# Slots of 576 columns, norm roots through DRAM, and a changed order at three places of a decoder layer

## The chip, the cores and the metric

The kernel runs on one core of one Trainium2 chip. The metric is the device time of one execution in microseconds (us). The kernel before takes 971.31 us (median of 3 runs, 971.28 to 971.34). The core has five engines with queues of their own: TensorE (PE in the profile; its weight loads are listed as PEld), VectorE (DVE), ScalarE (ACT), GpSimd (POOL) and SyncE (SP). Here SP only issues DMAs; POOL and ACT issue some as well.

## The reference

One layer of a hybrid decoder works on a prompt of 512 tokens and on 8 samples of 4 tokens each, with 1024 features. Cut to what the change touches:

```python
def _layer(x, ...):
    m, ... = _mixer(_rmsnorm(x, norm_mix_pre), ...)
    x = x + _rmsnorm(m, norm_mix_post)
    f, ... = _conv_ffn(_rmsnorm(x, norm_ffn_pre), ...)
    return x + _rmsnorm(f, norm_ffn_post), ...

def _rmsnorm(x, g):
    return x * rsqrt(mean(x * x, -1) + EPS) * g

def _mixer(h, ...):
    xr, q, k, v, g_lru, g_attn = split(h @ w_in)      # 1024, 1024, 256, 256, 1024, 1024 columns
    lru  = _rg_lru(_causal_dwconv(xr), ...)            # log_a = -8 * r * softplus(-lam)
    attn = _band_attention(q, k, v, ...)               # window 128, 8 query heads, 2 kv heads, bias, sinks
    return (sigmoid(g_lru) * (lru @ w_lru_o) + sigmoid(g_attn) * (attn @ w_attn_o)) @ w_out, ...
```

The samples attend over a cache of 128 keys and values each. Outputs are the two token arrays, the recurrent and convolution states and the key and value windows, all float32.

## The kernel before

**Tiles.** Activations lie with features on the 128 partitions and the 544 tokens (512 of the prompt, 32 of the samples) along the columns. A tile of that kind takes one of 53 slots of 568 columns (`SLOT`), so a slot is 2272 bytes long on each partition and every second one starts at an odd multiple of 32 bytes. Weights lie in `raw_*`, `wh_*`, `wl_*` tiles. Each float32 operand is split into a high and a low part (`hH`, `hL` of the normed input; `wh_in`, `wl_in` of the weights), and a product is three matmuls: high by high, low by high, high by low. DVE and ACT make the parts.

**Steps and ticks.** Work is cut into steps of one 128-column block of a weight matrix against one half of the tokens: 8 feature blocks by 3 products, 24 matmuls on 256 columns (half a=0) or 288 columns (half a=1), into one of three PSUM banks (`psm`; names `pm_first`, `pmin`). Behind each step stands a tick: it advances a clock by 1 and runs the side work that has become due. Side work is written as generators; `yield n` means that the next piece becomes due n ticks later (1 without a number). Lists named `mids`, `after`, `late` and `last` hold pieces for set places around a tick; the function given to `step` as `done` is such a piece and takes the finished bank. The order on PE, ACT, DVE and POOL in this part is exactly the order in which the code is written; each engine runs its own queue in order.

**Norm.** The input projection uses x times the gain. The reciprocal root of the mean square of each token is applied later: `rep` holds it, repeated on all partitions, and DVE multiplies it into the k, v, xr and gate columns (`scaled`, L171); q doesn't take it there, since the scores are scaled with `rq`. `norms` collects the squares in `ss` (one column for each block of tokens) and calls `roots` for the first two blocks (256 tokens) and later for the other three (288 tokens): DVE lays the roots on a diagonal (`dg`), a matmul of PE with `ones` spreads them over the partitions into `ps_rep`, and ACT copies that to `rep` (L554). A second small matmul into the same bank, `ohp` by `relx`, gives the rows of the bias table; they go by `rvec`, `rscr` and `rrep` through DRAM to the tables `btab` (L661, L686, L692, DMAs of POOL).

**Order of the blocks.** `qkv_order` lists the blocks of 128 columns: 8 to 15 are the query heads, 16 and 17 the keys, 18 and 19 the values. The first one is a step of its own (`pm_first`), and its `done` is put off by way of `after` and `mids`.

**Decay.** `params` computes the decay `cc`, `cneg` of the recurrence as a series, some 23 small instructions on POOL (L624 to L636). POOL also issues the DMAs `xdram` (L518), `kout`, `vout`, `knt`, `vnt` and `btab`.

**Samples.** `sample_attn(g)`, g = 0 and 1, loads cache rows, turns the keys by DVE (`kcT`, L893), and PE takes them for the scores `pss`.

**The end.** Finished features `ft` go out in three ways: the first token blocks come from PE in token order (`fg`, L1979), block 3 and half of block 2 are turned by PE (`yo`, L1887), the other half of block 2 is turned by DVE and leaves as 16 small DMAs (`yb_p`, L1866, list `pieces`, emptied by `send`), and the samples leave as 4 DMAs of POOL (`yb_s`, L1850, `samples_out`) once `y_blocks` has turned the last `ft`. The order there is written out at L2009 to L2043.

Of the kernel before, what the change touches and what calls it, by code (L numbers as in the profile page):

```python
# [11 lines left out]
F32 = mybir.dt.float32  # L12
F32R = mybir.dt.float32r
AF = mybir.ActivationFunctionType
ALU = mybir.AluOpType
# [31 lines left out]
SLOT = 568  # L47
# [76 lines left out]
def hawk_step(ctx, tc, I, O):  # L124
# [15 lines left out]
    cp = mixer.enter_context(tc.tile_pool(name="mixer_const", bufs=1))  # L140
    mixer.enter_context(tc.manual_schedule(engines={act.engine, dve.engine, pool.engine}))
# [16 lines left out]
    def SM(name, shape, tag="sm"):  # L158
        return smp.tile(shape, F32, tag=tag, name=name)
# [76 lines left out]
    qkv_order = (16, 18, 8, 9, 10, 11, 17, 19, 12, 13, 14, 15)  # L236
# [107 lines left out]
    def step(key, X, a, done, target=None, look=2, quick=False):  # L344

        first_ = key == order[0] and a == 0
        ps = first_ps if first_ else PM("pm" + "_".join(str(z) for z in key) + f"_{a}")
        if first_:
            pass
        elif quick:  # L350
            mmhalf(ps, key, X, a, range(4))
            now[0] += 0.5
            sides()
            mmhalf(ps, key, X, a, range(4, 8))
            done(a, ps)
        elif len(wunits) <= 2 * FIRST and a == 0 and key in order[1:FIRST]:
            mmhalf_low_last(ps, key, X, a)
        else:
            mmhalf(ps, key, X, a)
        tick(upto(key, a, look) if target is None else target, 0.5 if quick else 1)  # L360
        if first_:
            after.append(lambda: mids.insert(1, lambda: done(a, ps)))
        elif not quick:
            (last if len(wunits) <= 2 * FIRST and a == 0 else late).append(lambda: done(a, ps))
# [6 lines left out]
    rows_a = cp.tile([96, P], F32, name="rows_a")  # L371
# [31 lines left out]
    pvn = keep.tile([P, 24], F32, name="pvn")  # L403
# [25 lines left out]
    ss = cp.tile([P, 4, 5], F32, name="ss")  # L429
    dve.memset(ss, 1.0)  # L430
# [105 lines left out]

    def roots(i0, i1):
        dg = T(f"dg_{i0}")
        t0 = TOK[i0][0]
        spans = [(TOK[i][0] - t0, TOK[i][1], i) for i in range(i0, i1)]  # L540
        n = spans[-1][0] + spans[-1][1]
        last.append(lambda: xrstd(i0, i1))
        for o, w, i in spans:
            last.append(lambda o=o, w=w, i=i: dve.tensor_scalar(dg[:, o:o + w], ident[:, :w], ss[:, 1, i:i + 1], None,
                                                                ALU.mult))
        yield

        def spread_roots():
            ps = PX(f"ps_rep{i0}")
            mm(ps[:, 0:n], ones, dg[:, 0:n], True, True)  # L550
            if not i0:
                mm(ps[:NH, 256:256 + WIN], relx, ohp, True, True)
                ps_ohp.append(ps)
            act.copy(rep[:, t0:t0 + n], ps[:, 0:n])  # L554

        if i0:
            spread_roots()
        else:
            mids.insert(0, spread_roots)

    def norms():
        xsquare(0, 1, True)
        yield from roots(0, 2)
        yield
# [17 lines left out]
    rows_f = cp.tile([P, 2, P], F32, name="rows_f")  # L582
# [24 lines left out]
    def params():  # L607
# [15 lines left out]
        yield  # L623
# [255 lines left out]
    def sample_attn(g):  # L879
# [9 lines left out]
        yield 2  # L889
# [962 lines left out]
    def y_blocks(c):  # L1852
# [8 lines left out]
        if c == 3:  # L1861
            dst = yp[2 * P:3 * P, 0:512].rearrange("(b q) (c a d) -> a b q c d", b=4, a=4, d=32)
            src = yb["p"][:, 0:512].rearrange("p (b c d) -> p b c d", b=4, c=4)
            for a in range(4):
                for b in range(4):
                    pieces.append(lambda a=a, b=b: nc.sync.dma_start(out=dst[a, b], in_=src[32 * a:32 * a + 32, b]))  # L1866
            send(10)

    def send(n):
        for f in pieces[:n]:  # L1870
            f()
        del pieces[:n]
# [138 lines left out]
    r0 = rstd(0)  # L2011
    ps = tokens(1, 0)
# [3 lines left out]
    send(3)  # L2016
    gain = tokens_done(1, 0, ps)
    tokens_out(0, r0, 1)()
    send(len(pieces))
    while todo or side:  # L2020
        slot(0)
    samples_out()
# [56 lines left out]
```

## Time and profile before

| what | before |
|---|---|
| median of 3 runs | 971.31 us |
| the profiled execution | 971.4 us |
| its span in the trace | 969.6 us |
| instructions | 20080 |
| PE busy | 959.3 us, 99% of the span, 7598 matmuls |
| DVE busy | 762.3 us, 79% |
| ACT busy | 550.3 us, 57% |
| POOL busy | 166.3 us, 17% |
| granted TensorE clock, mean | 0.999 |
| HBM traffic | 118.21 MB read, 16.74 MB written, 139 GB/s |

All times of trace rows count from the start of the span; 1.8 us of the profiled execution lie outside it. A row of the timeline gives the start and the length of one instruction or of a run of like ones ("x3"), engine, line, operation, output and inputs without buffer numbers, and in brackets the idle time of the engine before it, with what ended it. Matmuls overlap, so the step from one start to the next, not the length shown, is what each takes from PE. "SPq", "ACTq" and the POOL rows of DMAs are the issue of a transfer, not the transfer itself.

### The profile page before, as it was taken

To read this page: it belongs to the slowest core of one execution; us is meant where nothing else is said; L and a number is where in the kernel's file an instruction comes from. 1 tells how busy PE (TensorE), PEld (TensorE's weight loads), DVE (VectorE), ACT (ScalarE), POOL (GpSimd) and SP (SyncE) were. 2 spreads that over 40 slices of the span, in tenths; PEclk is the share of its full clock that TensorE was granted. 3 is DMA by queue.
4 is the path that set the end of the run, shared out by engine and by line. 5 is a ranking of instruction groups with operands and counts; after the bars stand their busy time and mean duration, and the time that the engine had idled before them with its cause. 6 is when DMAs were issued, how large, how long until landed. Compare 5 with 4: busy or idle time off the path is not lost.

```text
span 969.6 us, 20080 instructions
## 1 busy us (share of the span) xinstructions
PE 959.3 (99%) x7598; PEld 951.6 (98%) x7598; DVE 762.3 (79%) x1626; ACT 550.3 (57%) x1342; POOL 166.3 (17%) x283
## 2 busy tenths in 40 slices
PE   9999999999999999999999999999999999999997
PEld 8999999999999999999999999999999999999996
DVE  5778888857858555689967878787888888888886
ACT  6544433467476425566867665555556565656642
POOL 2152000003406231230011110101011111111023
PEclk9999999999999999999999999999999999999999
DMA  7885436533334537235147575767667675859543
GB/s 221 235 240 164 149 90 155 157 94 88 92 104 152 172 102 196 66 124 178 46 108 196 132 188 141 183 154 171 166 154 195 143 200 135 203 130 234 178 147 92
DMA packets 247596, 147.26 MB, mean 152 GB/s; under 512 B 36324, under 2 KB 231788, under 8 KB 247468
## 3 DMA queue, kind: packets, MB, share of 16 engines
q1 hardware_dynamic: 237468, 124.15, 43.5%
q0 software_dynamic: 9824, 19.55, 12.0%
q10 hardware_dynamic: 208, 2.30, 0.6%
q8 instruction: 59, 0.97, 0.4%
q14 instruction: 37, 0.30, 0.1%
HBM read 118.21 MB, written 16.74 MB: 139 GB/s over the span
## 4 chain that ended last, share of the span: by engine, by line
PE 92%; DVE 5%; ACT 1%; issue 1%; DMA 0%; DVEq 0%; SPq 0%; POOL 0%; ACTq 0%; POOLq 0%
PE pmin L165 20%; PE pmdn L165 17%; PE pux L1531 16%; PE puy L1531 8%; PE pq L1531 6%; PE pmlo L165 5%; PE pmao L165 5%; PE pmout L165 4%; PE puz L1531 4%; PE pg L165 1%; PE pvp L165 1%; PE psc L165 1%; PE ptok L165 1%; DVE wl_e L168 1%; DMA pt<-pd 0%
## 5 line engine op out<-in xcount | busy, mean ns | idle before, releaser
L165 PE MATMUL pmin<-hH,wh_in 128*128 128x256 f32 (+1 forms) x568 | 163.9, 291 | 0.0
L165 PE MATMUL pmin<-hL,wh_in 128*128 128x256 f32 (+1 forms) x568 | 162.4, 288 | 0.0
L165 PE MATMUL pmin<-hH,wl_in 128*128 128x256 f32 (+1 forms) x568 | 159.1, 288 | 0.0
L165 PE MATMUL pmdn<-fH,wh_dn 128*128 128x256 f32 (+1 forms) x448 | 129.2, 288 | 0.0
L165 PE MATMUL pmdn<-fH,wl_dn 128*128 128x256 f32 (+1 forms) x448 | 128.8, 287 | 0.0
L165 PE MATMUL pmdn<-fL,wh_dn 128*128 128x256 f32 (+1 forms) x448 | 128.7, 287 | 0.0
L165 PEld LDWEIGHTS pmin<-hH,wh_in 128*128 128x128 f32 x568 | 107.2, 189 | 1.4 <-issue 1.2
L165 PEld LDWEIGHTS pmin<-hL,wh_in 128*128 128x128 f32 x568 | 107.2, 189 | 0.1
L165 PEld LDWEIGHTS pmin<-hH,wl_in 128*128 128x128 f32 x568 | 104.7, 188 | 0.2 <-issue 0.2
L177 DVE SCALAR_TENSOR_TENSOR uc<-u,fv,uc 128x560 f32<-128x560 f32 x128 | 101.9, 796 | 1.7 <-ACT uc L1562 1.2
L165 PEld LDWEIGHTS pmdn<-fH,wl_dn 128*128 128x128 f32 x448 | 84.4, 188 | 0.0
L165 PEld LDWEIGHTS pmdn<-fL,wh_dn 128*128 128x128 f32 x448 | 84.3, 188 | 0.1
L165 PEld LDWEIGHTS pmdn<-fH,wh_dn 128*128 128x128 f32 x448 | 84.2, 188 | 0.1
L1659 ACT COPY u<-pux 128x272 f32<-128x272 f32 x52 | 20.1, 386 | 87.2 <-PE pux L1531 87.2
L168 DVE TENSOR_TENSOR u<-puy,u 128x240 f32<-128x240 f32 (+2 forms) x78 | 24.6, 343 | 48.1 <-PE puy L1531 30.5
L174 DVE TENSOR_TENSOR ft<-ft,pmdn 128x256 f32<-128x256 f32 (+1 forms) x104 | 45.0, 433 | 16.6 <-PE pmdn L165 16.4
L283 ACT ACTIVATE wh_in<-raw_in 128x512 fp32r<-128x512 f32 x70 | 42.2, 624 | 21.3 <-issue 12.1
L290 DVE TENSOR_TENSOR wl_in<-raw_in,wh_in 128x512 fp32r<-128x512 f32 x70 | 47.8, 693 | 1.0 <-ACT wh_in L283 1.0
L1562 ACT ACTIVATE uc<-u,fv 128x560 f32<-128x560 f32 x64 | 48.1, 755 | 0.0
L781 ACT ACTIVATE s<-s,st 128x256 f32<-128x256 f32 (+1 forms) x32 | 15.2, 476 | 54.5 <-DVE st L778 43.2
L168 DVE TENSOR_TENSOR wl_dn<-raw_dn,wh_dn 128x512 fp32r<-128x512 f32 x56 | 38.3, 683 | 3.2 <-ACT wh_dn L1480 3.2
L1469 POOL DMA_DIRECT2D raw_up_s<-raw_up_s x26 | 22.0, 848 | 92.6 <-DMA raw_up_s<-raw_up__11280 5.5
(745 smaller groups left out, 3368.7 us busy)
## 6 DMA issues: line engine op xcount, KB each, us to landing
raw_in<-in_w_in_dram SPq DMA_DIRECT2D x35, 512.0 KB
raw_dn<-in_w_down_dram SPq DMA_DIRECT2D x56, 256.0 KB
raw_up_s<-in_w_up_dram SPq DMA_DIRECT2D x25, 512.0 KB
raw_up_s<-raw_up_s POOLq DMA_DIRECT2D x26, 256.0 KB, 4.2
raw_ao<-in_w_attn_o_dram SPq DMA_DIRECT2D x8, 512.0 KB
raw_lo<-in_w_lru_o_dram SPq DMA_DIRECT2D x8, 512.0 KB
raw_out<-in_w_out_dram SPq DMA_DIRECT2D x8, 512.0 KB
pd<-pb SPq DMA_DIRECT2D x12, 256.0 KB
```

What stands on the lines that cost most here:

```text
L165: pe.matmul(out, l, r, start=start, stop=stop)
L168: dve.tensor_tensor(out=out, in0=a, in1=b, op=ALU.subtract)
L174: dve.tensor_tensor(out=out, in0=a, in1=b, op=ALU.add)
L177: dve.scalar_tensor_tensor(out=out, in0=a, scalar=s_, in1=b, op0=op0, op1=op1)
L283: act.activation(hl[0], raw, AF.Copy)
L290: (eng or dve).tensor_tensor(out=hl[1], in0=raw, in1=f32(hl[0]), op=ALU.subtract)
L781: act.activation(s3[:, j, :], s3[:, j, :], AF.Exp, bias=ng[:, j:j + 1], accum_out=sm[:, j:j + 1])
L1469: pool.dma_start(out=w["p4"], in_=w["p2"], accum_op=ALU.add)
L1531: pe.matmul(ps[:, :HN], w, x, start=start and k == 0 and i == 0, stop=stop and k == 3 and i == 2, skip_group_check=True)
L1562: act.activation(yt[j][:, 0:FLATU], u[:, 0:FLATU], AF.Copy, scale=fv[:, j:j + 1])
L1659: act.copy(e[nm_], z)
```

## The change

1. **Slots.** `SLOT` goes from 568 to 576 columns (2304 bytes); the small tiles of the tags `sm` and `st` get a pool of their own for the mixer, `rows_a` and `rows_f` become parts of one temporary tile `rows`, and `pvn` and `ss` are padded to 32 columns. With that all operands start at multiples of 64 bytes.
2. **Order of the blocks.** Three query heads come ahead of the first keys and values, and the first step's `done` is no longer put off.
3. **Roots.** `dg`, its matmuls and the copies to `rep` go. DVE turns `ss` (`ssT`), POOL writes each block's roots into a row in DRAM (`rrow`), and one more DMA of POOL reads the row back into all partitions of `rep`. The matmul for the bias rows stays, with a bank of its own (`ps_ohp`).
4. **Decay.** The series starts 14 ticks after its inputs in place of 1.
5. **Samples.** The keys of the second group (g = 1) become due half a tick sooner.
6. **The end.** The loop that finishes the features, the samples' output and three of the `yb_p` pieces, now on POOL, stand ahead of the second block's products.

```diff
-SLOT = 568
+SLOT = 576
...
+    msp = mixer.enter_context(tc.tile_pool(name="mixer_small", bufs=4))
...
     def SM(name, shape, tag="sm"):
-        return smp.tile(shape, F32, tag=tag, name=name)
+        return (msp if tag in ("sm", "st") else smp).tile(shape, F32, tag=tag, name=name)
...
-    qkv_order = (16, 18, 8, 9, 10, 11, 17, 19, 12, 13, 14, 15)
+    qkv_order = (8, 9, 10, 16, 18, 11, 17, 19, 12, 13, 14, 15)
...
         tick(upto(key, a, look) if target is None else target, 0.5 if quick else 1)
-        if first_:
-            after.append(lambda: mids.insert(1, lambda: done(a, ps)))
-        elif not quick:
+        if not quick:
             (last if len(wunits) <= 2 * FIRST and a == 0 else late).append(lambda: done(a, ps))
...
-    rows_a = cp.tile([96, P], F32, name="rows_a")
+    rows = T("rows")
+    rows_a = rows[0:96, 0:P]
...
-    ss = cp.tile([P, 4, 5], F32, name="ss")
-    dve.memset(ss, 1.0)
+    ss_ = cp.tile([P, 32], F32, name="ss")
+    ss = ss_[:, 0:20].rearrange("p (z i) -> p z i", z=4)
+    ssT = cp.tile([P, 32], F32, name="ssT")
+    dve.memset(ss_, 1.0)
...
+    rrow = drp.tile([1, 5 * P], F32, name="rrow")
+
+    def bias_rows():
+        ps = PX("ps_ohp")
+        mm(ps[:NH, 256:256 + WIN], relx, ohp, True, True)
+        ps_ohp.append(ps)
+
     def roots(i0, i1):
-        dg = T(f"dg_{i0}")
         t0 = TOK[i0][0]
...
         last.append(lambda: xrstd(i0, i1))
-        for o, w, i in spans:
-            last.append(lambda o=o, w=w, i=i: dve.tensor_scalar(dg[:, o:o + w], ident[:, :w], ss[:, 1, i:i + 1], None,
-                                                                ALU.mult))
-        yield
-
-        def spread_roots():
-            ps = PX(f"ps_rep{i0}")
-            mm(ps[:, 0:n], ones, dg[:, 0:n], True, True)
-            if not i0:
-                mm(ps[:NH, 256:256 + WIN], relx, ohp, True, True)
-                ps_ohp.append(ps)
-            act.copy(rep[:, t0:t0 + n], ps[:, 0:n])
...
+        last.append(lambda: dve.transpose(ssT, ss_))
+        columns = ssT.rearrange("(a c) q -> c a q", c=32)
+        for i in range(i0, i1):
+            dst = rrow[0, i * P:(i + 1) * P].rearrange("(a q) -> a q", q=32)
+            last.append(lambda i=i, dst=dst: pool.dma_start(out=dst, in_=columns[5 + i]))
+        end = TOK[i1 - 1][0] + TOK[i1 - 1][1]
+        last.append(lambda: pool.dma_start(out=rep[:, t0:end], in_=rrow[0, t0:end].partition_broadcast(P)))
+        yield
...
         dve.reciprocal(lz, lz)
-        yield
+        yield 14
         pmul = lambda o, x, y: pool.tensor_tensor(out=o, in0=x, in1=y, op=ALU.mult)
...
-        yield 2
+        yield 2 - 0.5 * g
         kb4 = kb.rearrange("p (k b x) -> p k b x", k=NKV, b=4)
...
     r0 = rstd(0)
+    while todo or side:
+        slot(0)
+    samples_out()
+    send(3, pool)
     ps = tokens(1, 0)
     yo = [rows_t(3, (0,))]
     tokens_out(0, r0, 0)()
     yo[0]()
-    send(3)
+    send(len(pieces))
     gain = tokens_done(1, 0, ps)
     tokens_out(0, r0, 1)()
-    send(len(pieces))
-    while todo or side:
-        slot(0)
-    samples_out()
     gain()
```

The diff doesn't show where the moved pieces come to stand. The first place is POOL's queue in the first 60 us, before the change: behind three fillings of tables (`lt`, `stage`, `rvec`) come the DMAs of the bias tables, those of keys and values, and the series.

```order
L658 MEMSET rvec 8x384
L661 DMA rscr<-rvec 8x384
L686 DMA rrep_294<-rscr 128x768
L692 DMA btab_470<-rrep_294 128x2x256
L686 DMA rrep_295<-rscr 128x768
L692 DMA btab_678<-rrep_295 128x2x256
L732 DMA out_dram<-kout_790 128x128
L758 DMA out_dram<-vout_797 128x128
L686 DMA rrep_296<-rscr 128x768
L667 COPY lt<-rel_287 32x8 x16
L518 DMA xdram<-xn_249 128x544
L624 TENSOR_TENSOR lz<-lz,la 128x8
```

The same place of POOL's queue in the changed kernel:

```order
L656 MEMSET rvec 8x384
L553 DMA rrow<-ssT 4x32 x2
L555 DMA rep<-rrow 128x256
L659 DMA rscr<-rvec 8x384
L684 DMA rrep_298<-rscr 128x768
L690 DMA btab_473<-rrep_298 128x2x256
L684 DMA rrep_299<-rscr 128x768
L553 DMA rrow<-ssT 4x32 x3
L555 DMA rep<-rrow 128x288
L690 DMA btab_676<-rrep_299 128x2x256
L684 DMA rrep_300<-rscr 128x768
L665 COPY lt<-rel_291 32x8 x16
```

Seven DMAs have come in: two and one ahead of `rscr`, three and one between `rrep` and `btab` of the second table. `kout` and `vout` come later, and the series (`lz`, `cc`) now follows the last `btab`.

The second place is DVE's queue around 170 us, at the softmax of the last block of four heads (`st_3`, `s_3`), before:

```order
L171 TENSOR_TENSOR xr_2676<-pmin_0_2593,rep 128x256
L177 SCALAR_TENSOR_TENSOR xc_2494<-xr_2433,pv,xc_2494 128x568
L174 TENSOR_TENSOR st_3_2639<-st_3_2639 128x2
L787 RECIPROCAL st_3_2639<-st_3_2639 128x2
L789 TENSOR_SCALAR s_3_2637<-s_3_2637,st_3_2639 128x256 x2
L893 STREAM_TRANSPOSE kcT_2696<-cache_win_k_2581 128x2x2x128
L893 STREAM_TRANSPOSE kcT_2698<-cache_win_k_2581 128x2x2x128
L290 TENSOR_TENSOR wl_in_2674<-raw_in_2378,wh_in_2673 128x512
L171 TENSOR_TENSOR xr_2676<-pmin_1_2648,rep 128x256
```

The same place of DVE's queue in the changed kernel:

```order
L172 TENSOR_TENSOR xr_2677<-pmin_0_2594,rep 128x256
L178 SCALAR_TENSOR_TENSOR xc_2495<-xr_2434,pv,xc_2495 128x568
L891 STREAM_TRANSPOSE kcT_2684<-cache_win_k_2582 128x2x2x128
L891 STREAM_TRANSPOSE kcT_2686<-cache_win_k_2582 128x2x2x128
L175 TENSOR_TENSOR st_3_2640<-st_3_2640 128x2
L785 RECIPROCAL st_3_2640<-st_3_2640 128x2
L787 TENSOR_SCALAR s_3_2638<-s_3_2638,st_3_2640 128x256 x2
L291 TENSOR_TENSOR wl_in_2675<-raw_in_2379,wh_in_2674 128x512
L172 TENSOR_TENSOR xr_2677<-pmin_1_2649,rep 128x256
```

The two `kcT` have passed the four instructions of the softmax; `wl_in` and `xr` stand behind all of them in both.

The third place is the end of POOL's queue, before, where the last of the additions to `ft` are followed by the samples' output:

```order
L1837 TENSOR_TENSOR ft_7387<-ft_7387,x1r_13122 128x288
L1837 TENSOR_TENSOR ft_7493<-ft_7493,x1r_13124 128x288
L1837 TENSOR_TENSOR ft_7623<-ft_7623,x1r_13126 128x288
L1837 TENSOR_TENSOR ft_7725<-ft_7725,x1r_13128 128x288
L1850 DMA out_dram<-yb_s 256x1x32 x4
```

The same place of POOL's queue in the changed kernel:

```order
L1835 TENSOR_TENSOR ft_7389<-ft_7389,x1r_13124 128x288
L1835 TENSOR_TENSOR ft_7495<-ft_7495,x1r_13126 128x288
L1864 DMA out_dram<-yb_p 32x4x32
L1835 TENSOR_TENSOR ft_7625<-ft_7625,x1r_13128 128x288
L1864 DMA out_dram<-yb_p 32x4x32
L1835 TENSOR_TENSOR ft_7727<-ft_7727,x1r_13130 128x288
L1864 DMA out_dram<-yb_p 32x4x32
L1848 DMA out_dram<-yb_s 256x1x32 x4
```

Three `yb_p` pieces have come in between the additions; SP's queue has lost three at its end, and the four `yb_s` stand directly behind what turns the samples, where before other work was written in between.

More of the change, by code (lines that the diff above doesn't have):

```diff
@@ L402, in hawk_step @@
     pv = keep.tile([P, 96], F32, name="pv")
-    pvn = keep.tile([P, 24], F32, name="pvn")
+    pvn = keep.tile([P, 32], F32, name="pvn")[:, 0:24]
     pw = PM("ps_warm")
@@ L535, in hawk_step @@
     ps_ohp = []
+    rrow = drp.tile([1, 5 * P], F32, name="rrow")
[3 more added lines that the diff above has]
+        ps_ohp.append(ps)
     def roots(i0, i1):
-        dg = T(f"dg_{i0}")
         t0 = TOK[i0][0]
-        spans = [(TOK[i][0] - t0, TOK[i][1], i) for i in range(i0, i1)]
-        n = spans[-1][0] + spans[-1][1]
         last.append(lambda: xrstd(i0, i1))
-        for o, w, i in spans:
-            last.append(lambda o=o, w=w, i=i: dve.tensor_scalar(dg[:, o:o + w], ident[:, :w], ss[:, 1, i:i + 1], None,
-                                                                ALU.mult))
-        yield
-        def spread_roots():
-            ps = PX(f"ps_rep{i0}")
-            mm(ps[:, 0:n], ones, dg[:, 0:n], True, True)
-            if not i0:
-                mm(ps[:NH, 256:256 + WIN], relx, ohp, True, True)
-                ps_ohp.append(ps)
-            act.copy(rep[:, t0:t0 + n], ps[:, 0:n])
[L556 to L559, printed above, removed]
+        last.append(lambda: dve.transpose(ssT, ss_))
[5 more added lines that the diff above has]
+        last.append(lambda: pool.dma_start(out=rep[:, t0:end], in_=rrow[0, t0:end].partition_broadcast(P)))
+        yield
     def norms():
@@ L563, in norms @@
         yield from roots(0, 2)
+        mids.insert(0, bias_rows)
         yield
@@ L581, in hawk_step @@
     fv = keep.tile([P, 256], F32, name="fv")
-    rows_f = cp.tile([P, 2, P], F32, name="rows_f")
+    rows_f = rows[:, P:3 * P].rearrange("p (z q) -> p z q", z=2)
     fw = I["ffn_conv_w"].rearrange("o t (k p) -> (o t k) p", p=P)
@@ L1865, in y_blocks, with send @@
                 for b in range(4):
-                    pieces.append(lambda a=a, b=b: nc.sync.dma_start(out=dst[a, b], in_=src[32 * a:32 * a + 32, b]))
+                    pieces.append(lambda q, a=a, b=b: q.dma_start(out=dst[a, b], in_=src[32 * a:32 * a + 32, b]))
             send(10)
-    def send(n):
+    def send(n, q=nc.sync):
         for f in pieces[:n]:
-            f()
+            f(q)
         del pieces[:n]
```

## The prediction

> **What bounds the kernel now.** I read the busy times first, then the chain that ended last, then PE's own waits.
>
> ```profile
> PE 959.3 (99%) x7598; PEld 951.6 (98%) x7598; DVE 762.3 (79%) x1626; ACT 550.3 (57%) x1342; POOL 166.3 (17%) x283
> PE 92%; DVE 5%; ACT 1%; issue 1%; DMA 0%; DVEq 0%; SPq 0%; POOL 0%; ACTq 0%; POOLq 0%
> ```
>
> PE is busy for 99% of the span and carries 92% of the chain. An edit therefore counts in three ways only: it takes matmuls off PE, it makes or ends a wait of PE, or it changes what lies before PE's first or behind its last matmul. DVE's 762.3 us matter only where PE waits for DVE. All waits of PE that the profile lists are these (waiting tile, then who ended it: us in total, times, longest):
>
> ```profile
> PE pm_first L165 <- DVE wh_in L285: 1.2, 1, 1.2
> PE ps_warm L165 <- POOL ones L219: 1.0, 1, 1.0
> PE pvp L165 <- ACT tH L834: 0.5, 1, 0.5
> PE pvp L165 <- DVE tL L168: 0.2, 1, 0.2
> PE pmdn L165 <- DVE wl_dl L168: 0.2, 1, 0.2
> ```
>
> They come to 3.1 us. Of them, `pm_first` and `ps_warm` lie ahead of everything that the change touches, and `pmdn` is far behind it. Only the 0.7 us of `pvp`, near 175 us, have an edit beside them. So there is little to win by ending waits, and much more could be lost by making one.
>
> **The roots: matmuls off PE.** The timeline of PE where `rep` is made, for the first two blocks and then for the other three:
>
> ```profile
> 16.71 0.59 PE L165 MATMUL ps_rep<-dg,ones 128*128 128x256 f32 x2
> 17.23 0.39 PE L165 MATMUL ps_rep<-ohp,relx 128*8 128x128 f32 x2
> ...
> 33.67 0.65 PE L165 MATMUL ps_rep<-dg,ones 128*128 128x288 f32 x2
> 33.94 0.51 PE L165 MATMUL pmin<-hH,wh_in 128*128 128x288 f32 x1
> 34.28 0.30 PE L165 MATMUL pmin<-hL,wh_in 128*128 128x288 f32 x1
> 34.42 0.30 PE L165 MATMUL pmin<-hH,wl_in 128*128 128x288 f32 x1
> 34.55 0.29 PE L165 MATMUL pmin<-hH,wh_in 128*128 128x288 f32 x1
> ```
>
> The first `ps_rep` costs the step from 16.71 to 17.23, 0.52 us; the bias matmul behind it stays. At the second, the next step's second matmul starts at 34.28. At the ordinary step of 0.13 us (34.42 to 34.55) it would have started at 33.80 without `ps_rep`, so this one costs 0.48. Together **-1.0 us**. If the bias matmul keeps some cost of changing kind, it is -0.8; if a little more of the disturbed step goes, -1.2.
>
> **The roots: what takes their place.** `rep` now takes a transposition, a first hop (DMAs into `rrow`) and a second (one DMA back to all partitions). The trace has such hops of POOL, on the way of the bias table, the spread of the landing times for the tile `rscr`, and the window in which the first hop will lie (last but one number: busy share of the DMA engines, here full):
>
> ```profile
> 18.98 0.69 POOL L661 DMA_DIRECT2D rscr<-rvec  x1 [6.70 <-DVE rvec L660]
> 21.33 0.57 POOL L686 DMA_DIRECT2D rrep<-rscr  x1 [1.66 <-DMA rscr<-rvec]
> 25.81 0.74 POOL L692 DMA_DIRECT2D btab<-rrep  x1 [3.91 <-DMA rrep<-rscr]
> DMA to landing us min/median/max: 2.0/4.7/6.6
> 16.00:18.00 2.00, 2.00 (x15) 1.45 (x14) 0.00 (x0) 0.34 (x2) 0.00 (x0) 1.00 1.15 242
> ```
>
> From issue to the dependent issue the first took 2.35 us (21.33 less 18.98), the second 4.48. Unknown is what a hop h of the new chain takes; the bounds are the 2.0 and 6.6 of the last row, and I take its median, 4.7. When `rep` is needed follows from the queue of DVE, and from PE's use of the banks:
>
> ```profile
> 14.19 0.48 DVE L544 TENSOR_SCALAR dg<-ident,ss 128x128 f32<-128x128 f32 x2
> 27.62 1.79 DVE L177 SCALAR_TENSOR_TENSOR hL<-ps_tb,pv,hH 128x288 fp32r<-128x288 f32 x4 [1.05 <-ACT hH L455]
> ...
> 32.77 0.63 DVE L544 TENSOR_SCALAR dg<-ident,ss 128x128 f32<-128x128 f32 x3
> 40.06 0.47 DVE L177 SCALAR_TENSOR_TENSOR s<-psc,rq,btab 128x256 f32<-128x256 f32 x1
> 44.12 0.46 DVE L168 TENSOR_TENSOR qL<-pmin,qH 128x288 fp32r<-128x288 f32 x1 [1.47 <-ACT qs L712]
> 48.74 0.30 PE L165 MATMUL pmin<-hH,wh_in 128*128 128x288 f32 x1
> ```
>
> First `rep`: the roots are there at 14.19. Transposed in some 0.2, with two issues of `rrow` and one of `rep` at 0.57 each, the two hops start from 16.1, so `rep` is there at 16.1 + 2h = 25.5. Its first reader is `ks`, which now stands in DVE's queue right ahead of the four `hL` that began at 27.62, behind queries that don't need `rep`. To leave those where they are it must start by 27.2. So h may be 5.5, and the median leaves 1.7 us. Behind a late `ks` those four `hL` are late too, and PE's second half of the tokens reads them.
>
> Second `rep`: from 32.77, with 0.2 and four issues, the start is 35.2, and `rep` is there at 35.2 + 2h = 44.6. The key step of the second half has moved back by two places, and its `ks` comes to stand near 44.1, so DVE may wait half a microsecond. What counts is PE: the bank that this `ks` empties is taken again three steps later, by the 288-column step that begins at 48.74, and no weights are queued on DVE behind `ks` that a step before that one needs. So `ks` has until 48.3, and h may be 6.5. The bias rows on POOL, now behind the first `rep`, are later or sooner by about 1 us; their first table, issued at 25.81 and landed 6.6 later at most, is read first at 40.06. I put all this at **0**; with h = 6.6 for every hop, the first would be 2.1 us late and the second 0.1: +2.2.
>
> **The order of the blocks** itself adds and removes no matmul. The transposition of the last keys and of the values passes some steps to the rear on PE, and DVE's and ACT's shares of q, k and v change places: 0. What it does is to give the first `rep` the time that was just used.
>
> **The decay.** Twenty-three small instructions of POOL pass some twelve DMA issues.
>
> ```profile
> 51.94 0.20 POOL L624 TENSOR_TENSOR lz<-lz,la 128x8 f32<-128x8 f32 x1 [0.78 <-DVE st L174]
> 59.70 0.23 POOL L636 TENSOR_SCALAR cc<-cc 128x8 f32<-128x8 f32 x1
> 85.84 0.77 POOL L692 DMA_DIRECT2D btab<-rrep  x1
> 93.49 0.10 POOL L952 MEMSET xr<- 128x3 f32 x1 [6.88 <-DVE pb L823]
> ```
>
> The series takes 8.0 us (51.94 to 59.93). Moved behind the last `btab`, it starts near 86.6, and POOL's next instruction at 93.49 had 6.88 us of idle time before it. So it can be late by about 1 us, for three columns that are cleared. The `xdram` copies leave sooner. That hides the 8.0 us; without the idle time POOL would pass 1.2 us on (86.6 + 8.0 - 93.49) to its own clearing, not to PE: 0.
>
> **The samples' keys.** The only place where PE waits and the change acts, on DVE and then ACT:
>
> ```profile
> 171.37 1.30 DVE L893 STREAM_TRANSPOSE kcT<-cache_win_k 128x512 f32<-128x512 f32 x2
> 172.59 0.65 DVE L290 TENSOR_TENSOR wl_in<-raw_in,wh_in 128x512 fp32r<-128x512 f32 x1
> 173.16 0.51 DVE L171 TENSOR_TENSOR xr<-pmin,rep 128x256 f32<-128x256 f32 x2
> ...
> 173.77 0.86 ACT L963 ACTIVATE xc<-xr,pv 128x568 f32<-128x568 f32 x1 [2.68 <-DVE xr L171]
> 174.53 0.61 ACT L834 ACTIVATE tH<-pt 128x512 fp32r<-128x512 f32 x1
> ```
>
> `pvp` waits for `tH`, which stands on ACT behind `xc`, which waits 2.68 us for `xr`, which stands on DVE behind `wl_in` and the two `kcT`. The change puts `kcT` ahead of four softmax instructions; all six still stand ahead of `wl_in` and `xr`. The same sum of work ends at the same time: **0**, between -0.7 (the two waits gone) and +0.7 (the two doubled).
>
> **The slots.** Slots of 2272 bytes start by turns on a multiple of 64 bytes and 32 behind one, and the parts of `h` take both. Yet the matmuls that read them follow one another every 0.13 us all along (34.28, 34.42, 34.55), and so do their neighbours. If the start mattered to PE, the steps would alternate. 0. [...]
>
> **The end.** PE's last matmuls start at 961.54; behind it come the last squares, `fg` and the last transfers.
>
> ```profile
> 961.54 1.04 PE L1884 MATMUL pyo<-ident,ft 128*128 128x128 f32 x8
> 962.17 2.31 POOL L1850 DMA_DIRECT2D out_dram<-yb_s  x4 [5.97 <-DVE fg L171]
> L1979 SPq DMA_DIRECT2D out_dram<-fg x4: 351/378/768, 959.1 to 964.6; - x4
> ...
> q0 software_dynamic: 64, 0.07, 16.2%
> ...
> 965.50:966.50 1.00, 0.00 (x0) 0.00 (x0) 0.00 (x0) 0.00 (x0) 0.00 (x0) 1.00 1.05 402
> 967.50:968.50 1.00, 0.00 (x0) 0.00 (x0) 0.00 (x0) 0.00 (x0) 0.00 (x0) 0.57 0.12 43
> ```
>
> The queue row is of the 3 us from 964.5 to 967.5; in the windows the number before the last is the DMA engines' busy share. They are full (1.05) until the last `fg` lands near 967.6, and 16.2% of the 3 us, 0.49, is POOL's queue, that is `yb_s`. Issued some 3 us sooner, it is out of the way: **-0.45 us**, between 0 (if the last transfer waits for its own packets) and -1.0 (if it then lands 2.0 us, the shortest landing above, after its issue at 964.6). On DVE the samples' turning moves ahead of one `fg`, with the same sum before the last products.
>
> **Sum.** -1.0 - 0.45 and zeros: -1.45 us. The profiled execution took 971.4 (span 969.6 and 1.8 outside it), 0.09 above the median of 971.31. By the median that is 971.31 - 1.45 = **969.9 us**.
>
> **The rivals.** A measurement of this kernel can tell 0.2% (1.94 us) from no change: below 969.37 is faster, above 973.25 slower.
>
> *A, the waits end too.* If the samples' order also ends the 0.7 us of `pvp` and the last transfer lands after its 2.0 us (-1.0), the sum is -2.7: 968.6. For it: the edits stand just there, and a rearranged queue can start ACT sooner. Against it: the rows above leave the sum ahead of `xr` as it was.
>
> *B, the slots count.* One nanosecond off each second of 7598 matmuls is 3.8 us, and the total then 966.1. Against it stand the even steps.
>
> *C, nothing comes through.* PE gets ahead by 1 us near 34 us and loses it where it next meets something with its own time, such as `pvp`, which waits for DVE's work: 971.0 to 971.3. For it: DVE is full for 10 us before `pvp`. Against it: DVE itself starts from PE's results, and loses five `dg` instructions.
>
> *D, `rep` comes too late (slower).* Its place is `ks` on DVE, with `hL` and a bank of PE behind it. For it: the DMA engines are full when the first hop starts. It decides from h = 5.5 us for the first `rep` and 6.5 for the second. At h = 7.5, a little above any landing quoted, they are 3.9 and 1.9 us late, and -1.45 + 5.8 gives 975.7. Against it: the median of 4.7, for transfers much larger than these. [...]
>
> **How the numbers follow.** Forecast 0.46, A 0.29, B 0.05, C 0.12, D 0.08. Faster is A and B, 0.34; within 0.2% the forecast and C, 0.58; slower is D, 0.08. The range takes in the forecast, C and nearly all of A, with the bounds on PE's gain, the tail and `pvp` below (-1.2 - 1.0 - 0.7: 968.4) and the slowest hops above (-1.45 + 2.2: 972.1): 968.3 to 972.1, leaving out B and D.
>
> **What would show it.** PE has no `ps_rep<-dg` and its 2 matmuls fewer in the order; `ks` waits for the DMA of `rep` by under 1 us, and no new wait of PE names `hL`, `ks` or `kL`; the waits of `pvp` stay near 0.7; in the last 3 us POOL's queue has no packets, and the span ends about 0.4 us sooner after PE's last matmul. I am wrong if `rep` shows up in PE's chain, or if steps of equal width become shorter.

## The result, and the profile after

| kernel | median of 21 runs | lowest to highest |
|---|---|---|
| before | 971.36 us | 970.92 to 971.75 |
| changed | 972.59 us | 971.20 to 974.28 |

The ratio is 1.0014, with a 95% interval of 1.0008 to 1.0020. The change is slower by about 1.2 us, and above the range that the prediction gave. It also does what no term of the prediction had: the times of one and the same kernel now spread over 3.1 us, where they spread over 0.8. One kernel further down (changed, pad 64, roots on PE) had two executions far off, of 1516 us at a granted clock of 0.58 and of 5349 us; the first of them is its only trace, so its row leaves both out and nothing is read from its trace.

The profiled execution of the changed kernel took 971.2 us, with a span of 969.2; it happens to be the shortest of the 21. So its rows show where the kernel is led by other work, but not the whole loss. Its chain that ended last, by engine, and the two rows of the hardware queue that carries the weights, after and before:

```profile
PE 83%; DVE 11%; ACT 3%; issue 2%; DMA 1%; DVEq 0%; POOL 0%; ACTq 0%; POOLq 0%
q1 hardware_dynamic: 237036, 124.10, 45.8%
```

```profile
q1 hardware_dynamic: 237468, 124.15, 43.5%
```

PE's share of the chain fell from 92% to 83%, and DVE's rose from 5% to 11%. And nearly the same transfers (124.10 MB in 237,036 packets, before 124.15 in 237,468) now take 45.8% of the DMA engines' time in place of 43.5%. The waits of PE in the changed kernel:

```profile
PE ps_warm L166 <- POOL ones L220: 1.0, 1, 1.0
PE pvp L166 <- ACT tH L832: 0.4, 1, 0.4
PE pmin L166 <- DVE qL L169: 0.4, 1, 0.4
PE pm_first L166 <- DVE wh_in L286: 0.3, 1, 0.3
PE pvp L166 <- DVE tL L169: 0.2, 1, 0.2
PE pst_f L166 <- DVE accx L175: 0.2, 1, 0.2
PE pq L1529 <- DVE b11L L169: 0.2, 1, 0.2
PE pmdn L166 <- DVE wl_dl L169: 0.2, 1, 0.2
```

New are `pmin` waiting for `qL` of DVE and, by 0.2 us each, `pst_f` and `pq`. (`pm_first` waits 0.3 us here and 1.2 in the kernel before, but a second trace of the kernel before has 0.3 too, with its matmuls at the same times.) How PE comes to wait there is told by the chain in order of time (start, length, what), between 40 and 104 us:

```profile
40.06 5.42 DMA rep<-rrow
45.58 0.46 DVE ks L172
...
57.85 0.69 DVE vL L169
58.54 0.20 DVE vout L755
...
92.07 0.43 DVE qL L169
...
99.53 0.27 ACT qH L708
99.83 0.44 DVE qL L169
100.31 3.42 PE pmin L166 x24
```

From the DMA of the second `rep` the chain goes to `ks`, and then from DVE to ACT and back through the softmax for 54 us, until PE at last takes over at 100.31. In the kernel before, PE itself was the chain there. Matching each matmul of the two traces by its tiles and its place among the matmuls of these tiles, I read how far PE is ahead: 1.6 us at 44 us (the two `ps_rep` gone, and 0.5 us of turning keys and values that now comes later), 1.0 us once that is done, and 0.4 us *behind* at 101 us. The lead was taken back between 85 and 101 us, at three steps (0.4, 0.3 and 0.7 us). From there PE falls behind by another 0.9 us until 350 us and gains 1.7 until its end, though it waits for nothing new there: the step from one matmul to the next has changed (at 256 columns from 117.9 to 119.5 ns, by the traces below).

### The profile page after: what moved, and what is told of

Same layout as the page of the kernel before. It is cut to its first block, busy times and chain, and to the rows that moved or that the text cites. A ratio compares the mean times of both kernels' runs of the same rounds, so it can differ in the third digit from the quotient of the medians.

```text
span 969.2 us, 20090 instructions
## 1 busy us (share of the span) xinstructions
PE 959.4 (99%) x7594; PEld 951.5 (98%) x7594; DVE 761.3 (79%) x1623; ACT 549.4 (57%) x1340; POOL 173.3 (18%) x293
## 3 DMA queue, kind: packets, MB, share of 16 engines
q1 hardware_dynamic: 237036, 124.10, 45.8%
## 4 chain that ended last, share of the span: by engine, by line
PE 83%; DVE 11%; ACT 3%; issue 2%; DMA 1%; DVEq 0%; POOL 0%; ACTq 0%; POOLq 0%
PE pmdn L166 18%; PE pux L1529 16%; PE pmin L166 13%; PE puy L1529 8%; PE pq L1529 6%; PE pmlo L166 5%; PE pmao L166 5%; PE pmout L166 4%; PE puz L1529 4%; PE pg L166 1%; ACT s L779 1%; DVE st L774 1%; DVE s L178 1%; PE pvp L166 1%; DVE wl_e L169 1%
## 5 line engine op out<-in xcount | busy, mean ns | idle before, releaser
L175 DVE TENSOR_TENSOR ft<-ft,pmdn 128x256 f32<-128x256 f32 (+1 forms) x104 | 45.0, 434 | 16.3 <-PE pmdn L166 16.2
L291 DVE TENSOR_TENSOR wl_in<-raw_in,wh_in 128x512 fp32r<-128x512 f32 x70 | 47.8, 693 | 0.6 <-ACT wh_in L284 0.6
```

The source lines that it names most:

```text
L175: dve.tensor_tensor(out=out, in0=a, in1=b, op=ALU.add)
L291: (eng or dve).tensor_tensor(out=hl[1], in0=raw, in1=f32(hl[0]), op=ALU.subtract)
```

## The experiments

Each kernel was timed beside the kernel before on the same chip. "Pad" kernels leave some bytes of SBUF unused ahead of the slots.

| kernel | median | lowest to highest | ratio (95%) |
|---|---|---|---|
| changed, again | 973.02 | 971.51 to 974.02 | 1.0018 (1.0009 to 1.0027) |
| changed, roots on PE | 971.70 | 970.77 to 972.94 | 1.0005 (0.9997 to 1.0014) |
| slots only | 972.60 | 971.93 to 974.63 | 1.0015 (1.0007 to 1.0024) |
| slots only, pad 64 | 971.27 | 970.69 to 972.19 | 1.0000 (0.9991 to 1.0009) |
| before, pad 192 | 971.92 | 971.63 to 973.60 | 1.0009 (1.0000 to 1.0017) |
| changed, pad 64 | 971.94 | 970.46 to 972.26 | 1.0003 (0.9994 to 1.0011) |
| changed, pad 64, roots on PE | 972.12 | 970.85 to 972.48 | 1.0006 (0.9997 to 1.0015) |
| changed, pad 64, extra hop | 974.87 | 973.60 to 975.98 | 1.0041 (1.0026 to 1.0055) |
| changed without slots | 972.31 | 971.73 to 974.57 | 1.0014 (1.0005 to 1.0023) |
| slots 32 behind 64, rest at 256 | 971.70 | 971.26 to 972.00 | 1.0004 (0.9995 to 1.0013) |
| order only | 971.77 | 971.35 to 971.98 | 1.0004 (0.9995 to 1.0013) |
| decay, keys, end only | 971.18 | 970.79 to 972.27 | 0.9999 (0.9990 to 1.0008) |
| changed, pad 64, order and roots undone | 971.27 | 970.71 to 971.94 | 1.0001 (0.9992 to 1.0009) |

The kernel before was at 971.2 to 971.4 each time. A median's own interval is near 0.9 us, so single differences below that are read from the traces and not from this table.

### Is it the slots, or the late `rep`?

The changed kernel and the kernel before were profiled a second time. Then the roots alone were put back on PE:

```diff
 def roots(i0, i1):
-    ... ssT, rrow, rep through DRAM
+    ... dg, ps_rep, act.copy(rep, ps_rep)
```

and the kernel before was given part 1 alone:

```diff
-SLOT = 568
+SLOT = 576
 ...
+    msp = ... "mixer_small"; rows = T("rows"); ss and pvn padded to 32 columns
```

> The changed kernel once more, for a second trace. Theory L (late rep): in the first trace the second rep landed at 45.5 us, ks on VectorE waited 2.67 us for it, and TensorE lost 0.22, 0.16 and 0.59 us at 83, 91 and 99 us; where the landing varies, ks starts at another time than 45.58 and these three losses move with it: about 1 us of loss for each us that ks is later. Median near 972.6, spread over 2 to 3 us. Theory S (slots): the step from matmul to matmul is again 119.6 ns at 256 columns, 125.0 at 272 and 131.7 at 288, as in the first trace (before: 117.9, 125.5, 132.8). Rival to S: the steps belong to the execution and not to the kernel, and differ from trace to trace.

> The kernel before once more, for a second trace. Theory S: steps of 117.9, 125.5 and 132.8 ns again at 256, 272 and 288 columns. Rival: other steps, so that the difference between the first two traces says nothing on the slots. Time 971.3.

> The changed kernel with the roots spread by TensorE as before (dg, ps_rep, copy by ScalarE), all else of the change kept. Theory L: ks of the second half doesn't wait for a DMA, the three losses near 83, 91 and 99 us go, the two ps_rep cost 1.0 us; median 971.0 to 971.8, and the spread of the executions falls from 3 us to under 1. Rival M (the moved blocks): the rearranged VectorE queue is late by itself; losses and spread stay, median 973 or more.

> The kernel before with part 1 alone (slots of 576 columns, the small tiles' pools and padding). Theory S: steps of 119.6, 125.0 and 131.7 ns, and a median lower by some 0.9 us (the drift of TensorE's rows against those of before from 130 to 953 us in the first two traces, +0.8 then -1.7), 970.4. Forecast's zero: steps as before and 971.3.

The second traces settle the steps first. From the start of one matmul to that of the next, the mean over some 1,700 matmuls of 256 columns, 3,300 of 272 and 1,700 of 288 is 117.9, 125.5 and 132.8 ns in both traces of the kernel before, and 119.5, 125.0 and 131.7 in both of the changed one. They belong to the kernel. `a4_slots_only` has 119.5, 125.3 and 131.7, so the slots make them. The prediction's "0 for the slots" was wrong in this. But the sum nearly cancels: the expected gain of 0.9 us did not come, and the time went *up* by 1.3 us, with most of the spread of the changed kernel (2.7 us of 3.1). The rows of that trace that differ are the landing times of POOL's transfers for the up-projection, which add one raw weight tile to another (`raw_up_s`; before: 3.3, 4.2, 6.0), the weights' queue, and the instruction of ACT that waits for such a sum at the end of that phase:

```profile
DMA to landing us min/median/max: 3.4/4.5/7.6
...
q1 hardware_dynamic: 237468, 124.15, 45.8%
...
883.64 0.63 ACT L1483 ACTIVATE wh_s_p<-raw_up_s 128x512 fp32r<-128x512 f32 x1 [1.37 <-DMA raw_up_s<-raw_up_s]
```

A sum of weights that lands late at 884 us stops ACT, and PE behind it (`pux` waits 0.3 us for `wl_s_p`; PE's matmuls are 0.6 us later behind this place than ahead of it). In the trace with the roots on PE the same wait is 2.64 us on ACT, and 0.7 on PE (matmuls 1.0 us later). Before, ACT ran through at this place. At the end the slots-only kernel loses once more: its span goes on for 7.96 us from the start of PE's last matmul, where the kernel before takes 7.28. The packets of the queue are the same, 237,468 of them; they only take longer.

The roots on PE brought 1.3 us back (973.02 to 971.70), as theory L (the late `rep`) wants, but the spread stayed above 2 us, which it does not want. The second trace of the changed kernel speaks against L as well: `ks` started 0.3 us sooner than in the first (45.27), and PE's waits for `qL` were 1.1 us and not 0.4.

### Where the weights land

The slots start at byte 19104 of a partition before and at 19136 after. 53 slots of 2272 bytes then end at 139520, which is 545 times 256. 53 slots of 2304 end at 141248, which is 192 more than 551 times 256. All that lies behind the slots, the split weights and the buffers into which the raw weights land, was moved with it (those of `raw_dn`, which had never been at a multiple of 256, from 128 behind one to 64). So four kernels set the two apart: columns as in the change or as before, landing at 0 or at 192 behind a multiple of 256.

```diff
 pv = keep.tile([P, 96], F32, name="pv")
+keep.tile([P, 16], F32, name="pad")      # 64 bytes; 48 columns for 192
```

> The changed kernel with 64 unused bytes put ahead of the slots, so that slots, split weights and the landing buffers of the weights all start at multiples of 256 bytes; in the changed kernel all of these start 192 behind such a multiple, before the landing buffers and most split weights started at one. Theory P (placement): the queue of weight transfers falls from 45.8% to 43.5% of the 16 DMA engines' time, the longest landing for raw_up_s from 7.6 to about 6.0 us, the median from 972.6-973.0 to about 971.7, with what the late rep costs remaining. Theory S (columns or 64-byte starts alone): nothing changes, 972.6 to 973.0 and 45.8%.

> The kernel before with 192 unused bytes ahead of the slots: slots still of 568 columns, but the landing buffers and split weights now start 192 bytes behind a multiple of 256, as in the changed kernel. Theory P: the queue's share rises to 45.8%, landings to 7.6 us, the median to about 972.6 with a spread of over 2 us. Theory S: 971.3, 43.5%, spread under 1 us. The matmul steps stay at 117.9, 125.5, 132.8 ns if they hang on the slots, and move to 119.5, 125.0, 131.7 if they hang on where the weights lie.

> The changed kernel with the roots on TensorE as before and the 64 bytes: both suspected losses taken away. P with L (late rep): 971.7 less 1.3, about 970.4, spread under 1 us. If the two losses are one and the same, 971.7 stays.

> The kernel before with slots of 576 columns and the 64 bytes. P: the 1.3 us of the slots go, 971.3 or below, 43.5%, spread under 1 us. S: 972.6 again.

The queue of the weights in the kernel before with its landing moved by 192, and in the slots-only kernel with its landing moved back by 64:

```profile
q1 hardware_dynamic: 237468, 124.15, 45.8%
```

```profile
q1 hardware_dynamic: 237468, 124.15, 43.5%
```

Share and landing times (7.6 us against 6.3 at the longest) follow the place, in both directions, and the time with them: 971.92 for the kernel before once its landing is off, 971.27 for the slots once it is right again. The matmul steps do not: 117.8 and 132.8 ns in the first, 119.5 and 131.7 in the second. In the first, ACT again waits for `raw_up_s` near 882 us (1.50 us), PE is 0.7 us later behind it, and the span goes on for 7.74 us from PE's last matmul. So the loss of part 1 goes with the place where the weights land, shown both ways: 1.3 us by moving it back, 0.6 by moving it off (972.6 was expected there). A pad moves the slots and the split weights too, but the share is 43.5 to 43.7% in all kernels below that land at a multiple of 256, with slots at three different kinds of start. The mean packet is 523 bytes (124.15 MB over 237,468). What the place changes in the writing of such a packet is in no trace, so why the place counts is open. The rows show 5% more time for the same packets (45.8% in place of 43.5%), in five traces with the landing off against eleven with it right.

The changed kernel gained 1.1 us by the pad. With the roots on PE as well, 970.4 was expected and 972.12 came, so the two losses do not add up. That miss was the hint that theory L was not the whole story.

### What makes the lead vanish

Three kernels: one more hop in front of the second `rep`; the change with slots of 568 columns and its landing at a multiple of 256; slots of 576 columns that all start 32 behind a multiple of 64. The changed kernel with the pad was profiled a second time.

```diff
+row = rrow2 if i0 else rrow
+if i0:
+    last.append(lambda: pool.dma_start(out=rrow2[0, t0:end], in_=rrow[0, t0:end]))
-last.append(lambda: pool.dma_start(out=rep[:, t0:end], in_=rrow[0, t0:end] ...))
+last.append(lambda: pool.dma_start(out=rep[:, t0:end], in_=row[0, t0:end] ...))
```

> The changed kernel with the 64 bytes, and one more hop (from a row in DRAM to another) ahead of the second rep: the suspected wait doubled. Its ks then starts near 50 us in place of 45.3. Theory L (TensorE loses what ks is late): 971.9 + 4.5 = 976.4. Theory C (from about 53 to 105 us a chain of VectorE and ScalarE at the softmax sets the pace with a rhythm of its own, which takes back TensorE's lead whether ks is late by 2.7 us or not; in the changed kernel VectorE's lateness of 2.8 us at ks against the one with roots on TensorE is 0.6 by 59 us): the chain takes up some 2 to 3 us and the rest is lost, 973.5 to 974.5.

> The kernel before with slots of 576 columns, all slots starting 32 bytes behind a multiple of 64 and split weights and landing buffers at multiples of 256. If the matmul steps hang on starts at multiples of 64, they return to 117.9, 125.5 and 132.8 ns; if they hang on all operands starting alike, they stay at 119.5, 125.0 to 125.3 and 131.7. Transfers to weights as in the kernel before, 43.5%; time near 971.3 in both cases.

> The changed kernel with slots of 568 columns again and 224 unused bytes, so that landing buffers and split weights start at multiples of 256 as before: all parts but the first. Placement taken out: 43.5%, steps of 117.9, 125.5, 132.8 ns. Theory C: TensorE's lead of 1.6 us at 44 us is gone by 105 us but for 0.3; with 0.1 from the end, 970.9, spread under 1 us. Forecast of the parts 2 to 6: 969.9.

> The changed kernel with the 64 bytes once more, for a second trace. Its times fell into two groups (970.5 to 970.9 and 971.6 to 972.3), and the first trace, of 971.94, had steps of 126.7 ns in the 272-column stretch from 425 to 490 us, where other traces have 124.4: 0.8 us over some 380 matmuls. Theory T (two rhythms per execution): a look in the lower group shows 124.4, one in the upper 126.7. Rival: the steps there are the program's, 126.7 in every look.

Without the slots, parts 2 to 6 cost 1.0 us, where theory C had wanted a small gain and the forecast a large one. Both missed. The extra hop costs 2.9 us more than the kernel it was added to, less than theory L wanted (976.4) and a little more than theory C (974.5 at most). In its trace, the shortest of its five executions, `ks` and PE's new wait are:

```profile
46.21 0.46 DVE L172 TENSOR_TENSOR ks<-pmin,rep 128x288 f32<-128x288 f32 x1 [6.43 <-DMA rep<-rrow]
...
PE pmin L166 <- DVE qL L169: 2.1, 3, 1.4
```

Only 0.6 to 2.0 us later than in the five other traces with the roots through DRAM (`ks` at 44.2 to 45.6), and yet PE's waits for `qL` were 2.1 us, where those five have 0.4 to 1.1.

Then I set DVE's rows of all traces against those of before, by their place in the queue. In every kernel with the new order, with the roots by DRAM *or* on PE, DVE jumps by 2.2 us at one point, near 54 us; in every kernel with the old order it does not. At 66 us this leaves it 1.1 to 3.1 us late. That is not yet the lateness with which it reaches 97 us. In between, near 71 us, DVE writes the tile `pb` (softmax rows) again, and waits there until the transfer `pd` has taken the last ones out of it (1.06 us in the trace with the order alone, 0.2 in the first one of the changed kernel with the pad; in the first one of the changed kernel it comes 0.04 us behind the landing and waits for nothing):

| trace | DVE late at 66 us | `pd` has landed at | DVE late at 97 us | PE late at 101 us |
|---|---|---|---|---|
| before (for comparison) | | 65.82 | | |
| changed, pad 64, second trace | 1.1 | 71.01 | 2.3 | 0.2 |
| changed, pad 64 | 2.2 | 71.15 | 2.5 | 0.3 |
| changed without slots | 1.4 | 71.17 | 2.5 | 0.3 |
| changed | 2.5 | 71.26 | 2.6 | 0.4 |
| changed, roots on PE | 1.9 | 71.42 | 2.7 | 0.7 |
| changed, again | 2.2 | 71.81 | 3.1 | 1.0 |
| changed, pad 64, extra hop | 3.1 | 73.03 | 4.4 | 2.2 |

(The landing is read from the start of the `pt` that waits for it.) DVE's lateness at 97 us is in every row the landing less 68.7 us, whatever it was at 66. And PE is late by what DVE is late less some 2.2 us, with one exception. With the roots on PE, PE waits for no `qL`: it had lost 0.5 us at 34 us, where the second `ps_rep` waits for DVE, and had no lead with which to make this up. So in these traces the lead is used up down to the 2.2 us by which DVE may be late, and what DVE is late beyond that PE pays.

### The order by itself

```diff
-qkv_order = (16, 18, 8, 9, 10, 11, 17, 19, 12, 13, 14, 15)
+qkv_order = (8, 9, 10, 16, 18, 11, 17, 19, 12, 13, 14, 15)
 ...
-if first_: after.append(... done ...)
```

was put alone into the kernel before, parts 4 to 6 alone into another copy of it, and in the changed kernel with the pad parts 2 and 3 were undone.

> The kernel before with part 2 alone: three query heads ahead of the first keys and values, the first step's done not put off; roots on TensorE, slots of 568. Theory O (the order costs): turning out the last keys and the values (kout, vL with its wait for vH, vout: 2.6 us on VectorE) now falls at 54 to 58 us into a stretch where VectorE and ScalarE run without slack until 105 us; in every trace with the new order VectorE's rows are 2.3 to 2.7 us later from there on (0.1 with the old order), and TensorE, which can take about 2.2, ends up behind: TensorE some 0.5 us later than before at 99 us, time 971.6 to 972.3. Forecast (the order costs nothing): 971.3, and no jump.

> The kernel before with parts 4, 5 and 6 alone (decay later, samples' keys sooner, the end's order). Forecast: 971.3 - 0.45 = 970.9, all of it behind TensorE's last matmul. By the traces so far (span against TensorE's last row, kernels with the new end against those with the old): -0.1, 971.2. Spread under 1 us.

> The changed kernel with the 64 bytes, parts 2 and 3 undone (old order, roots on TensorE): slots, decay, keys and end. Theory O: VectorE's rows at 94 us are 0.1 us off those of before, not 2.3 to 2.7; TensorE loses nothing at 83 to 99 us; times 970.6 to 971.2 in the lower group and 0.9 more in the upper, as the slots' two rhythms at 425 to 490 us go. If the order is innocent, it stays at the 971.9 of the kernel with 64 bytes.

What moved, in DVE's timeline before and with the order alone:

```profile
45.85 0.28 DVE L731 COPY kout<-pk 128x128 f32<-128x128 f32 x1
46.05 0.68 DVE L168 TENSOR_TENSOR vL<-pv,vH 128x512 fp32r<-128x512 f32 x1
46.65 0.28 DVE L757 COPY vout<-pv 128x128 f32<-128x128 f32 x1
```

```profile
55.05 0.28 DVE L729 COPY kout<-pk 128x128 f32<-128x128 f32 x1
56.80 0.69 DVE L168 TENSOR_TENSOR vL<-pv,vH 128x512 fp32r<-128x512 f32 x1 [1.48 <-ACT vH L752]
57.41 0.28 DVE L755 COPY vout<-pv 128x128 f32<-128x128 f32 x1
```

Three instructions and a wait of 1.48 us for ACT came from 46 us to 55 us. The `pd` behind them is issued later by this, and lands later still; before, and with the order alone:

```profile
61.30 0.34 SPq L826 DMA_DIRECT2D pd<-pb  x1
65.82 1.83 SPq L831 DMA_DIRECT2D pt<-pd  x4
...
68.77 0.70 DVE L823 STREAM_TRANSPOSE pb<-s 128x512 f32<-128x512 f32 x1
```

```profile
62.71 0.34 SPq L824 DMA_DIRECT2D pd<-pb  x1
71.26 1.74 SPq L829 DMA_DIRECT2D pt<-pd  x4
...
71.30 0.71 DVE L821 STREAM_TRANSPOSE pb<-s 128x512 f32<-128x512 f32 x1 [1.06 <-DMA pd<-pb]
```

Before, `pd` was out of the way 3 us ahead of DVE's next `pb`. In the kernels with the new order it takes 7.5 to 8.6 us to land. Why it takes so long there is open (in the second trace of the kernel before it took 7.3 and was still in time; of the traces with the old order, one has DVE waiting for it, by 0.3 us). What this does 30 us on is one row, the `qL` behind which PE waits: before, with the order alone, with the order undone, and in the changed kernel:

```profile
97.22 0.42 DVE L168 TENSOR_TENSOR qL<-pmin,qH 128x256 fp32r<-128x256 f32 x1 [1.38 <-ACT qH L710]
```

```profile
99.79 0.42 DVE L168 TENSOR_TENSOR qL<-pmin,qH 128x256 fp32r<-128x256 f32 x1 [1.38 <-ACT qH L708]
```

```profile
97.43 0.42 DVE L169 TENSOR_TENSOR qL<-pmin,qH 128x256 fp32r<-128x256 f32 x1 [1.38 <-ACT qH L715]
```

```profile
99.83 0.42 DVE L169 TENSOR_TENSOR qL<-pmin,qH 128x256 fp32r<-128x256 f32 x1 [1.38 <-ACT qH L708]
```

The order alone puts it 2.57 us later, and the changed kernel 2.61: the order alone is enough for it. Theory O holds in this, though not in its way there: DVE is late by the landing of `pd`, and not by the length of the three instructions. In time the order alone came out at 971.77, 0.5 above the kernel before but inside the interval. In its trace PE loses 0.3 us at the second `ps_rep`, 0.3 us at `qL`, and 0.4 us behind 105 us without a wait.

Whether this is the 1.0 us of parts 2 to 6 is argued and not shown. By the table, where `rep` or `pd` lands late in one execution and not in the next, PE pays for it (1.8 us more where `pd` landed at 73.03 us in place of 71.26); and the spreads agree (0.6 us with the order alone, 2.8 with parts 2 to 6 together). But executions without a trace can't be asked, and the one trace without the slots, whose 972.31 is just its median, says otherwise: there PE is 0.3 us late at 105 us and 1.1 us at its end. The other 0.8 us came later, a little at a time and without a new wait, and what made them is open. Part 3 in the old order was not run.

With parts 2 and 3 undone the changed kernel is at 971.27. No version beat the kernel before by what can be told apart.

### The matmul rhythm

The chain also gives long runs of matmuls without a wait. 336 with halves of 256 and 288 columns, then 216 and 384 of 272 columns, before:

```profile
224.36 42.00 PE pmao L165 x336
368.95 27.16 PE pmout L165 x216
437.82 48.15 PE pq L1531 x384
```

In the changed kernel with the pad, first trace (971.94 us):

```profile
224.95 42.27 PE pmao L166 x336
370.31 26.88 PE pmout L166 x216
439.04 48.63 PE pq L1530 x384
```

and the last of the three in its second trace (970.69 us):

```profile
438.88 47.80 PE pq L1530 x384
```

Slots that all start at multiples of 64 bytes make `pmao` slower by 0.6% and `pmout` faster by 1.0%. In `pq` one and the same kernel runs at 124.5 ns a matmul in one execution and at 126.6 in another (47.80 and 48.63 over 384), as theory T had it. The nine traces of kernels with such slots have one of the two (five 47.8, four 48.63), and never a value between. These 0.8 us are a part of the spread that the slots bring; how the other executions, which left no trace, divide was not seen. With slots 32 behind a multiple of 64 the steps are 117.2, 125.6 and 133.4 ns: neither those of before nor those of the change. Both expectations for that kernel fail, and what sets the step stays open.

## Why the prediction was wrong, point by point

1. **The slots, put at 0: the step that failed most.** It asked whether the engines read a slot faster, and never where the longer slots push what lies behind them. Most landing buffers of the weights left their multiple of 256 bytes; the weights' packets took 5% longer (45.8% of the DMA engines' time in place of 43.5%), and the median rose by 1.3 us (slots only, 972.60, against 971.27 with 64 bytes of padding). Also its reason was too narrow: that steps do not alternate within the kernel before does not say that their mean stays when all slots start alike (117.9 ns before and 119.5 with the new slots, at 256 columns).
2. **The order of the blocks, put at 0: the second step that failed.** The prediction said of it that "DVE's and ACT's shares of q, k and v change places: 0". It counted instructions, which are the same, and not the stretch they fall into. DVE was 2.2 us later from 54 us on, the softmax rows `pd` left later and landed at 71.0 to 71.8 us in place of 65.8 (73.0 with the extra hop), DVE waited for them (1.06 us with the order alone), and PE for DVE at 100 us. PE lost 0.3 us there with the order alone, and 1.4 us between 85 and 101 us in the changed kernel.
3. **The roots off PE, -1.0 us.** Mechanism and size were right: PE was 1.0 us ahead at 60 us. That it stays ahead was wrong. Rival C described this ("loses it where it next meets something with its own time"), but put it near 175 us and gave it 0.12; it happens between 85 and 101 us.
4. **The hops.** The first `rep` was in time, as predicted: its `ks` started at 25.31 without waiting for it. The second was predicted for 44.6 and landed at 45.5; `ks` waited 2.67 us and not half a microsecond, as DVE came to it sooner (42.9) than its old place had said. The bound by the PSUM bank, 48.3, was kept, so rival D's place was wrong: a late `rep` does not hurt at the bank but 40 to 55 us on. It delays DVE, and with DVE the `pd` that lands at 71 us, and PE pays from the 2.2 us on that DVE may be late.
5. **Decay and keys, 0.** As predicted: `pvp` waits 0.6 us in place of 0.7, and parts 4 to 6 alone are at 971.18. (Of its own sums, 86.6 + 8.0 - 93.49 is 1.1 us and not 1.2, and the lower bound of the range is 968.4 by its terms.)
6. **The end, -0.45 us: the right mechanism, mis-sized.** POOL's packets did leave the last 3 us, 0.6% of the engines' time there in place of 16.2. But from the start of PE's last matmul the changed kernel gains only 0.1 us (7.21 and 7.28). In its timeline:

```profile
961.27 1.03 PE L1882 MATMUL pyo<-ident,ft 128*128 128x128 f32 x8
963.35 1.41 DVE L178 SCALAR_TENSOR_TENSOR fg<-fg,nst_t,xtok 128x512 f32<-128x512 f32 x2
```

   Before, the last `fg` started at 963.16, or 1.62 us behind the start of PE's last run at 961.54; now it starts 2.08 us behind. The turning of the samples, moved ahead on DVE, made the earlier `fg` late, and the last one with them: 0.46 us given back. "The same sum before the last products" was the failing step. The 0.1 us also sets a kernel with its landing off against one with its landing right. Among the traces with the landing off, the new end takes 7.14 to 7.21 us and the old one 7.74 and 7.96, so there it is worth 0.5 to 0.8; with the landing right the two ends take 7.03 to 7.32 and 7.00 to 7.39, and no gain can be told.

## What to carry to other kernels

When a buffer's size changes, write down the start addresses of everything behind it. Here the place that transfers land in cost 1.3 us and the place that an engine reads from did not show in the median: the longer slots took 972.60 us, and 971.27 with 64 bytes of padding, beside 971.2 to 971.4 for the kernel before. When work is moved on an engine that is not the bottleneck, ask which stretch it moves into, which transfers then leave later, and who waits for their landing. When the bottleneck engine gets ahead, ask where it next waits for others: here PE was 1.6 us ahead at 44 us and 0.4 us behind at 101 us, once it had waited for DVE.

## What the runs showed of the hardware that was not expected

- The same packets into SBUF take 45.8 to 45.9% of the DMA engines' time with most landing buffers 192 bytes behind a multiple of 256 (five traces), and 43.5 to 43.7% at one (eleven traces). POOL's 256 KB transfers for `raw_up_s` land after 4.5 to 4.6 us (median; longest 7.6 to 8.2) in place of 4.2 (6.0 to 7.2).
- The matmul step hangs on where the slots start: it goes from 117.9 to 119.5 ns at 256 columns (+1.4%) and from 132.8 to 131.7 at 288 (-0.8%) when all slots start at multiples of 64 bytes; with such slots the stretch `pq` takes either of two values, 124.5 or 126.6 ns, in executions of one kernel.
- A small round trip from SBUF through DRAM and back to all partitions took 11.2 us in the first trace of the changed kernel, while weights were loading (the second `rep`, from the issue of the last `rrow` at 34.3 to the landing at 45.5).
